# Four operand sums of a Strassen-like down projection, moved from VectorE to accumulating SBUF-to-SBUF transfers

## Chip, cores, metric

One NeuronCore of a Trainium2 chip runs the whole kernel. The metric is device time in microseconds, the median over runs of the same program. A profiled execution gives the trace; its times count from the first instruction (the span's start). Engines are named as in the profile: PE (TensorE matmul), PEld (its weight loads), DVE (VectorE), ACT (ScalarE), POOL (GpSimd), SP (SyncE). POOL and SP issue DMA transfers; those that accumulate into their destination are issued by POOL here.

## What is computed

One layer of a streaming encoder on 512 positions of 1024 channels, in float32. The part that matters here is the gated feed-forward block at the end, with 2816 hidden channels:

```python
h2 = rms_norm(x, norm_ffn[l])
act = jax.nn.silu(jnp.einsum('bsd,df->bsf', h2, w_ffn_gate[l])) * jnp.einsum('bsd,df->bsf', h2, w_ffn_up[l])
x = x + jnp.einsum('bsf,fd->bsd', act, w_ffn_down[l])
```

Before it come a combined input projection, a pooling mixer, a gated linear recurrence and stick-breaking attention, merged by gates, and an output projection. None of these is touched.

## The kernel before

Activations are held with channels on the 128 partitions and positions along the free dimension. A float32 product is made of three matmuls in a rounded 32-bit format: each operand is split into a high part (an ACT copy that rounds) and a low part (DVE: operand minus high part), and hi x hi, hi x lo and lo x hi are accumulated. A split of a weight set therefore costs an ACT copy and a DVE subtraction of 128x1024; a split of an activation block costs the same two of 128x512 for each chunk.

Large products use seven half-size products in place of eight (a Strassen-Winograd scheme). Sums of weights are formed in SBUF by accumulating transfers on POOL's queue or on DVE; sums of activations are formed on DVE.

**The feed-forward block.** The gate and up products run in eleven steps `c` (0 to 10, `DOWN` = 11), each giving `acts[c]`: a tile of 128 x 2 x 512, where the middle index is one of two 128-channel chunks. `finish_act` (L1404) ends the seven products of a step with `S4` for the first chunk and `S3` for the second. It multiplies both factors by `rb2`, the reciprocal RMS per position formed in `rms2`, applies Silu on ACT and multiplies. The last index of `acts` splits into two halves `j` of H = 256 positions.

**The down projection.** `acts[0]` is multiplied in the ordinary way (weights `fd`, tile `ps_d`, L274 to L276). `acts[1]` to `acts[10]` are the Strassen operand: block (i, j) is made of chunks of `acts[1+5i]` to `acts[5+5i]`, positions half j. `ablk(i, kh, j)` gives the pieces for one third `kh` of it: two tiles for kh 0 and 1, one for kh 2, five tiles of 128x512 in all. `split_d2(nm, kh, i, j)` splits such a piece for the product `nm`, on ACT (L1400) and DVE (L1401); its tiles are named `Bd` + product + kh (+ h or l), for instance `BdS20h`. The split of "11" is written during the last step of the gate and up products (`PRE`).

The seven products run in `DORDER` = 11, 12, S1, S2, S3, S4, 22, each with five weight sets n = 0 to 4 in the six pieces of `USE` (two output halves `q`), 120 matmuls of 256 columns at L1633 into `ps_dy` or `ps_dx`. Weight sets are split at L1379 (ACT, `whd`) and L1380 (DVE, `wld`); three split sets can be held at a time. `make_d` writes them ahead of the pieces: ahead of piece p of the first half, up to set p + 2. The raw weights:

- for "11" and "12", "22": sets of "11" are loaded into `DY` (tile `dw`), those of "12" and "22" into three raw buffers (tile `dr`, loaded by SP at L1549 when a buffer comes free);
- for the sums, `DX` is loaded with the block 21 and gets 22 added (S1), later 11 (S2) and 12 (S4); `DY` gets 21 added (S3). Each is an accumulating transfer of 512 KB that POOL issues at L1537, behind the split that has read the set (`NEXT`).

**The sums of activations.** Four sums are formed by `in_place` (L1570) on DVE, in the tiles of `acts` themselves: T1 = (0,0) - (0,1) in the place of (0,0), then T2, T4 in the same place, and T3 in the place of (0,1). Each needs five instructions of 128x512. `LATER[nm]` lists, for each product, which sums and splits are written between its pieces: two entries behind each piece of the first output half, one behind each of the second. T1 and the split of S1 stand in "11", T2 and the split of S2 in "12", T3 and the split of S3 in "S1", the split of S4 and T4 in "S2".

**What sets the order.** Each engine and each DMA queue runs its instructions in the order in which a scheduler put them before the run; semaphores hold an instruction back until its inputs are there, and everything behind it on that engine with it. The scheduler takes instructions by program order among those that it believes to be ready, so that a transfer written late can be issued early. `tc.keep_in_program_order` puts an instruction behind the one that was written just before it on its engine; `in_place` and the DVE part of `split_d2` (for products other than "11" and "12") use it, ACT parts and transfers do not.

Of the kernel before, what the change touches and what calls it, by code (L numbers as in the profile page):

```python
# [31 lines left out]
H = S // 2  # L32
# [34 lines left out]
def layer_kernel(ctx: ExitStack, tc: tile.TileContext, x, xt, vecs, w_in, w_qkv7, w_gate7, w_pool, w_rg, w_ig,  # L67
                 w_branch, w_br7, w_out, w_fd, w_gu7, w_fd7, out):
    nc = tc.nc
    act = nc.scalar.activation  # L70
    dve = nc.vector
# [332 lines left out]
    with ExitStack() as first:  # L404
# [394 lines left out]
        for t in VKQ:  # L799
            ps = {}  # L800
# [451 lines left out]
    with ExitStack() as ffn:  # L1252
# [6 lines left out]
        def small(name, bufs=1, tag=None, dt=F32):  # L1259
            return gp.tile([P, S], dt, tag=tag or name, name=name, bufs=bufs)  # L1260
# [3 lines left out]
        act(onesr, ones, AF.Copy)  # L1264
        sqsum = small("sqsum")
        rb2 = small("rb2")

        x1p = {}
        x1 = []

        def rms2():
# [14 lines left out]
            dve.tensor_tensor(rb2, rb2, ms, ALU.mult)  # L1286
            dve.tensor_scalar(rb2, rb2, -0.5, 1.5, ALU.mult, ALU.add)
            dve.tensor_tensor(rb2, rb2, t, ALU.mult)

# [97 lines left out]
        def ablk(i, kh, j):  # L1387
            return [acts[1 + 5 * i + 2 * kh + n][:, :, j * H:(j + 1) * H] for n in range(2 - kh // 2)]

        def split_d2(nm, kh, i, j):  # L1390

            pin = tc.keep_in_program_order if nm not in ("11", "12") else lambda i: None
            if kh < 2:
                h, l = g4([4, H], f"Bd{nm}{kh}h", F32R), g4([4, H], f"Bd{nm}{kh}l", F32R)
            else:
                t = g4([2, 2, H], f"Bd{nm}{kh}", F32R)
                h, l = t[:, 0], t[:, 1]
            for n, src in enumerate(ablk(i, kh, j)):
                ns = slice(2 * n, 2 * n + 2)
                act(h[:, ns, :], src, AF.Copy)  # L1400
                pin(dve.tensor_tensor(l[:, ns, :], src, h[:, ns, :].bitcast(F32), ALU.subtract))  # L1401
            DB[nm, kh] = h, l

        def finish_act(t, ps, a, sign):  # L1404

            dve.tensor_tensor(t, t, ps, ALU.add)
            for w in range(2):
                dve.tensor_tensor(t[:, w, :], t[:, w, :], rb2, ALU.mult)
            act(t[:, 0, :], t[:, 0, :], AF.Silu, scale=sign)
            if sign > 0:  # L1410
                dve.tensor_tensor(a, t[:, 0, :], t[:, 1, :], ALU.mult)
            else:
                dve.scalar_tensor_tensor(a, t[:, 1, :], sign, t[:, 0, :], ALU.mult, ALU.mult)


        PRE = ("S2", "S4", "22")
# [1 line left out]
        def seven(n):  # L1418
# [39 lines left out]
                dve.tensor_tensor(ah[1], acts[0], ah[0].bitcast(F32), ALU.subtract)  # L1458
            if c == DOWN - 1 and nm in PRE:
                split_d2("11", PRE.index(nm), 0, 0)  # L1460
            if nm == "S4":
                finish_act(tx, X, a[:, 0, :], 1.0)
            if nm == "S3":
                finish_act(ty, Y, a[:, 1, :], -1.0)

        T, Z, ah = {}, {}, []

# [97 lines left out]
                    dadd(m, n, buf)  # L1565
                dfetch(dmade[0] + 2)

        def in_place(dst, sign, op, other):
            return [lambda kh=kh: [tc.keep_in_program_order(
                dve.scalar_tensor_tensor(t, t, sign, o, ALU.mult, op)) for t, o in zip(ablk(dst[0], kh, dst[1]), ablk(other[0], kh, other[1]))]  # L1570
                    for kh in range(3)]

        def both(nm, i, j):
            return [lambda kh=kh: split_d2(nm, kh, i, j) for kh in range(3)]

# [3 lines left out]
                   lambda: [dload("21", n, DX) for n in range(5)],  # L1579
                   lambda: [dadd("22", n, DX) for n in range(5)]] + both("12", 1, 0)[:1])  # L1580

        LATER = {"11": both("12", 1, 0)[1:] + in_place((0, 0), 1.0, ALU.subtract, (0, 1)) + both("S1", 0, 0),
                 "12": in_place((0, 0), -1.0, ALU.subtract, (1, 1)) + both("S2", 0, 0),
                 "S1": in_place((0, 1), -1.0, ALU.add, (1, 1)) + both("S3", 0, 1),
                 "S2": both("S4", 1, 1) + in_place((0, 0), -1.0, ALU.subtract, (1, 0)),
                 "S3": both("22", 0, 0)}

        for e in range(2):
# [128 lines left out]
```

## Time and profile before

| | |
|---|---|
| median of 3 runs | 900.3 us (899.79 to 902.87) |
| the profiled execution | 900.52 us, of which the span of instructions is 898.7 us |
| granted PE clock, mean | 0.998 |
| accumulating transfers of weights in the down projection (POOL, 512 KB) | 20, median 8.0 us from issue to landing |
| loads of weights in the down projection (SP, 512 KB) | 20, medians 6.3 and 5.7 us |
| PE busy from 880 us to the end of the span | 15.35 of 19.00 us |

How to read it: a busy time is the union of an engine's instructions; an engine that is off the path may be idle without cost. In rows of a timeline the first two numbers are start and length in us, and the bracket gives the idle time ahead of the instruction and what ended it. In rows of groups, "x15: 680/682/684" are count and shortest, median and longest duration in ns. In the busy times by stretch, each stretch has its length, then busy time and number of instructions for each engine, then the granted PE clock, the share of the 16 DMA engines' time, and GB/s. In the chain of waits each piece is what the next one waited for.

### The profile page before, as it was taken

To read this page: it belongs to the slowest core of one execution; us is meant where nothing else is said; L and a number is where in the kernel's file an instruction comes from. 1 tells how busy PE (TensorE), PEld (TensorE's weight loads), DVE (VectorE), ACT (ScalarE), POOL (GpSimd) and SP (SyncE) were. 2 spreads that over 40 slices of the span, in tenths; PEclk is the share of its full clock that TensorE was granted. 3 is DMA by queue.
4 is the path that set the end of the run, shared out by engine and by line. 5 is a ranking of instruction groups with operands and counts; after the bars stand their busy time and mean duration, and the time that the engine had idled before them with its cause. 6 is when DMAs were issued, how large, how long until landed. Compare 5 with 4: busy or idle time off the path is not lost.

```text
span 898.7 us, 14578 instructions
## 1 busy us (share of the span) xinstructions
PE 891.1 (99%) x5731; PEld 802.4 (89%) x5731; DVE 736.7 (82%) x937; ACT 532.9 (59%) x747; POOL 106.7 (12%) x150
## 2 busy tenths in 40 slices
PE   9999999999999999999999999999999999998998
PEld 6888778888899888888888988999999999998998
DVE  7897897988786599967887685798888888998974
ACT  7554989556856556555664545655555555654642
POOL 1010002232332101000001100000010100121200
PEclk9999999999999999999999999999999999999999
DMA  9485347798582786634635864836666676887913
GB/s 342 141 309 150 114 132 210 220 299 244 179 262 71 234 234 192 218 118 145 214 93 154 190 179 164 258 81 174 169 148 176 162 169 201 211 210 205 196 39 117
DMA packets 83620, 164.59 MB, mean 183 GB/s; under 512 B 7904, under 2 KB 48864, under 8 KB 83552
## 3 DMA queue, kind: packets, MB, share of 16 engines
q1 hardware_dynamic: 68000, 107.29, 35.9%
q0 software_dynamic: 15408, 56.11, 28.2%
q8 instruction: 45, 0.74, 0.3%
q10 hardware_dynamic: 144, 0.26, 0.1%
q14 instruction: 23, 0.19, 0.1%
HBM read 143.19 MB, written 18.87 MB: 180 GB/s over the span
## 4 chain that ended last, share of the span: by engine, by line
PE 93%; DVE 3%; ACT 2%; DMA 1%; issue 1%; DVEq 0%; ACTq 0%; SPq 0%
PE ps_y L283 13%; PE ps_x L283 10%; PE ps_q L794 7%; PE ps_dy L1633 5%; PE ps_dx L1633 4%; PE ps_br L274 3%; PE ps_br L275 3%; PE ps_br L276 3%; PE ps_bY L1234 2%; PE ps_gy L283 2%; PE ps_gate L697 2%; PE ps_gate L276 2%; PE ps_bX L1234 2%; PE ps_gx L283 2%; PE ps_gate L274 2%; PE ps_gate L275 2%
## 5 line engine op out<-in xcount | busy, mean ns | idle before, releaser
L110 ACT ACTIVATE whi<-raw 128x1024 fp32r<-128x1024 f32 x61 | 64.6, 1059 | 73.3 <-PE ps_br L275 14.7
L111 DVE TENSOR_TENSOR wlo<-raw,whi 128x1024 fp32r<-128x1024 f32 x61 | 74.4, 1220 | 28.9 <-ACT whi L110 28.9
L111 DVE TENSOR_TENSOR wlo<-qw,whi 128x1024 fp32r<-128x1024 f32 x48 | 58.6, 1222 | 20.8 <-ACT whi L110 20.4
L110 ACT ACTIVATE whi<-qw 128x1024 fp32r<-128x1024 f32 x48 | 50.7, 1057 | 33.1 <-PE ps_q L794 18.7
L1379 ACT ACTIVATE wh<-w 128x1024 fp32r<-128x1024 f32 x34 | 36.2, 1064 | 49.4 <-PE ps_x L283 24.7
L1380 DVE TENSOR_TENSOR wl<-w,wh 128x1024 fp32r<-128x1024 f32 x34 | 41.6, 1223 | 7.3 <-ACT wh L1379 6.7
L1380 DVE TENSOR_TENSOR wl_S<-w,wh_S 128x1024 fp32r<-128x1024 f32 x30 | 36.6, 1220 | 12.1 <-ACT wh_S L1379 12.0
L1379 ACT ACTIVATE wh_S<-w 128x1024 fp32r<-128x1024 f32 x30 | 31.8, 1060 | 22.5 <-PE ps_y L283 19.8
L1379 ACT ACTIVATE whdS<-dw 128x1024 fp32r<-128x1024 f32 x20 | 21.3, 1064 | 22.1 <-PE ps_dy L1633 11.1
L1380 DVE TENSOR_TENSOR wldS<-dw,whdS 128x1024 fp32r<-128x1024 f32 x20 | 24.2, 1220 | 6.4 <-ACT whdS L1379 6.3
L1050 DVE TENSOR_TENSOR_SCAN E<-K,ahead 128x512 f32<-128x512 f32 (+3 forms) x32 | 25.3, 812 | 4.4 <-ACT K L1046 4.4
L274 PE MATMUL ps_br<-yHH,whi 128*128 128x512 f32 x64 | 25.3, 395 | 0.0
L274 PE MATMUL ps_lru<-HH,whi 128*128 128x512 f32 x64 | 25.2, 394 | 0.0
L274 PE MATMUL ps_br<-yph,whi 128*128 128x512 f32 x64 | 25.2, 394 | 0.0
L274 PE MATMUL ps_pool<-HH,whi 128*128 128x512 f32 x64 | 25.2, 393 | 0.0
L274 PE MATMUL ps_gate<-HH,whi 128*128 128x512 f32 x64 | 25.0, 391 | 0.0
L276 PE MATMUL ps_gate<-HH,wlo 128*128 128x512 f32 x64 | 25.0, 391 | 0.0
L275 PE MATMUL ps_br<-ypl,whi 128*128 128x512 f32 x64 | 25.0, 391 | 0.0
L276 PE MATMUL ps_br<-yph,wlo 128*128 128x512 f32 x64 | 25.0, 391 | 0.0
L275 PE MATMUL ps_br<-yHL,whi 128*128 128x512 f32 x64 | 25.0, 390 | 0.0
L276 PE MATMUL ps_br<-yHH,wlo 128*128 128x512 f32 x64 | 25.0, 390 | 0.0
L275 PE MATMUL ps_pool<-HL,whi 128*128 128x512 f32 x64 | 25.0, 390 | 0.0
(768 smaller groups left out, 3540.0 us busy)
## 6 DMA issues: line engine op xcount, KB each, us to landing
w<-in_w_gu_dram SPq DMA_DIRECT2D x44, 512.0 KB, 6.6
raw<-in_w_in_dram SPq DMA_DIRECT2D x31, 512.0 KB, 5.2
qw<-in_w_qkv_dram SPq DMA_DIRECT2D x24, 512.0 KB, 6.5
w<-in_w_gu_dram POOLq DMA_DIRECT2D x20, 512.0 KB, 7.3
dw<-in_w_down_dram POOLq DMA_DIRECT2D x20, 512.0 KB, 8.0
raw<-in_w_branch_dram SPq DMA_DIRECT2D x16, 512.0 KB, 4.2
qw<-in_w_qkv_dram POOLq DMA_DIRECT2D x12, 512.0 KB, 7.8
qd<-r POOLq DMA_DIRECT2D x12, 512.0 KB, 7.8
```

Of the source, the lines that this page charges most:

```text
L110: act(hi, raw, AF.Copy)
L111: dve.tensor_tensor(lo, raw, hi.bitcast(F32), ALU.subtract)
L274: nc.tensor.matmul(ps, lh, rh, start=start, stop=False, skip_group_check=skip)
L275: nc.tensor.matmul(ps, lh, rl, start=False, stop=False, skip_group_check=skip)
L276: nc.tensor.matmul(ps, ll, rh, start=False, stop=stop, skip_group_check=skip)
L283: nc.tensor.matmul(o, a_[a][:, w, k, :], b_[b][:, k, :], start=first and n == k == 0, stop=last and n == 2 and k == 3, skip_group_check=True)
L794: nc.tensor.matmul(ps[:, a, :], b_[:, k, ts_], a_[:, kk, :], start=first and n == k == 0, stop=n == 2 and k == 3, skip_group_check=True)
L1050: dve.tensor_tensor_scan(E[:, c0:c0 + n][:, ::-1], K[:, c0 + 1:c0 + n + 1][:, ::-1], ahead[:, S - n:][:, ::-1], 0.0, ALU.mult, ALU.add)
L1234: nc.tensor.matmul(o, ah[x_][:, w, k, :], b[k][y_], start=first_ and n == k == 0, stop=n == 2 and k == 3, skip_group_check=True)
L1379: act(h, src, AF.Copy)
L1380: dve.tensor_tensor(l, src, h.bitcast(F32), ALU.subtract)
L1633: nc.tensor.matmul(o, a_[a][:, w, k0 + k, :], b_[b][:, k, :], start=first and i == k == 0, stop=last and i == 2 and k == nk - 1, skip_grou ...
```

## The change

All four sums become accumulating transfers from SBUF to SBUF, issued by POOL: `dma_sum(dst, kh, other)` adds the block `other` into the block `dst`, one transfer of 128x512 (256 KB) for each tile. The transfers add, so two of the four blocks are written negated: `rbn` holds `rb2` with the second half of the positions negated (two ACT copies of 128x256 in `rms2`, in the place of `sqsum`), and `finish_act` multiplies the second factor by `rbn`; for steps from 6 on the sign of the product is turned as well. Blocks (0,1) and (1,0) then hold negated values. The splits "S2" and "12" read their block negated (ACT with a scale of -1, DVE with a scalar_tensor_tensor).

The places in the program change too: T1 is written directly behind the split of "11" for each kh, during the last step of the gate and up products; T2 behind the split of S1 for each kh, in "11"; T3, the split of S2 and T4 together for each kh, in "12". The lists for "S1" and "S2" keep splits alone.

```diff
+        rbn = sqsum
...
+            act(rbn[:, :H], rb2[:, :H], AF.Copy)
+            act(rbn[:, H:], rb2[:, H:], AF.Copy, scale=-1.0)
...
+        def dma_sum(dst, kh, other):
+            for t, o in zip(ablk(dst[0], kh, dst[1]), ablk(other[0], kh, other[1])):
+                nc.gpsimd.dma_start(t, o, accum_op=ALU.add)
...
             for n, src in enumerate(ablk(i, kh, j)):
                 ns = slice(2 * n, 2 * n + 2)
+                if nm in ("S2", "12"):
+                    act(h[:, ns, :], src, AF.Copy, scale=-1.0)
+                    pin(dve.scalar_tensor_tensor(l[:, ns, :], src, -1.0, h[:, ns, :].bitcast(F32), ALU.mult,
+                                                 ALU.subtract))
+                    continue
...
-        def finish_act(t, ps, a, sign):
+        def finish_act(t, ps, a, sign, first):
...
-            for w in range(2):
-                dve.tensor_tensor(t[:, w, :], t[:, w, :], rb2, ALU.mult)
+            for w, r in enumerate((rb2, rbn)):
+                dve.tensor_tensor(t[:, w, :], t[:, w, :], r, ALU.mult)
             act(t[:, 0, :], t[:, 0, :], AF.Silu, scale=sign)
-            if sign > 0:
+            if (sign > 0) == first:
                 dve.tensor_tensor(a, t[:, 0, :], t[:, 1, :], ALU.mult)
             else:
-                dve.scalar_tensor_tensor(a, t[:, 1, :], sign, t[:, 0, :], ALU.mult, ALU.mult)
+                dve.scalar_tensor_tensor(a, t[:, 1, :], -1.0, t[:, 0, :], ALU.mult, ALU.mult)
...
             if c == DOWN - 1 and nm in PRE:
                 split_d2("11", PRE.index(nm), 0, 0)
+                dma_sum((0, 0), PRE.index(nm), (0, 1))
...
-        def in_place(dst, sign, op, other):
-            return [lambda kh=kh: [tc.keep_in_program_order(
-                dve.scalar_tensor_tensor(t, t, sign, o, ALU.mult, op)) for t, o in zip(ablk(dst[0], kh, dst[1]), ablk(other[0], kh, other[1]))]
-                    for kh in range(3)]
...
-        LATER = {"11": both("12", 1, 0)[1:] + in_place((0, 0), 1.0, ALU.subtract, (0, 1)) + both("S1", 0, 0),
-                 "12": in_place((0, 0), -1.0, ALU.subtract, (1, 1)) + both("S2", 0, 0),
-                 "S1": in_place((0, 1), -1.0, ALU.add, (1, 1)) + both("S3", 0, 1),
-                 "S2": both("S4", 1, 1) + in_place((0, 0), -1.0, ALU.subtract, (1, 0)),
+        LATER = {"11": both("12", 1, 0)[1:] + [lambda kh=kh: (split_d2("S1", kh, 0, 0), dma_sum((0, 0), kh, (1, 1)))
+                                               for kh in range(3)],
+                 "12": [lambda kh=kh: (dma_sum((0, 1), kh, (1, 1)), split_d2("S2", kh, 0, 0), dma_sum((0, 0), kh, (1, 0)))
+                        for kh in range(3)],
+                 "S1": both("S3", 0, 1),
+                 "S2": both("S4", 1, 1),
                  "S3": both("22", 0, 0)}
```

More of the change, by code (lines that the diff above doesn't have):

```diff
@@ L1460, in seven @@
                 split_d2("11", PRE.index(nm), 0, 0)
+                dma_sum((0, 0), PRE.index(nm), (0, 1))
             if nm == "S4":
-                finish_act(tx, X, a[:, 0, :], 1.0)
+                finish_act(tx, X, a[:, 0, :], 1.0, c < 6)
             if nm == "S3":
-                finish_act(ty, Y, a[:, 1, :], -1.0)
+                finish_act(ty, Y, a[:, 1, :], -1.0, c < 6)
         T, Z, ah = {}, {}, []
```

## The prediction, as put on record

> **What bounds the kernel now.** I read the page first, then the waits of PE, the busy times by stretch for the down projection, PE's timeline there, and last the chain of waits in that stretch.
>
> ```profile
> span 898.7 us, 14578 instructions
> ...
> PE 891.1 (99%) x5731; PEld 802.4 (89%) x5731; DVE 736.7 (82%) x937; ACT 532.9 (59%) x747; POOL 106.7 (12%) x150
> ```
>
> PE is busy for 99% of the span, so VectorE time alone is worth nothing; only a stretch where PE is short of operands can be improved. The waits of PE name the one place behind the start where it stands still.
>
> ```profile
> PE ps_dx L1633 <- ACT whd L1379: 1.7, 2, 0.9
> ...
> PE ps_dx L1633 <- DVE wld L1380: 0.8, 1, 0.8
> ```
>
> L1633 is the down projection, ps_dx in its second product ("12"), and whd, wld are the two halves of its split weights. The busy times by stretch show what this place costs:
>
> ```profile
> core 0: us, PE busy (x) PEld busy (x) DVE busy (x) ACT busy (x) POOL busy (x), PEclk, DMA share, GB/s
> ...
> 784.00:800.30 16.30, 16.30 (x96) 14.45 (x95) 16.24 (x24) 8.70 (x13) 2.56 (x3) 1.00 0.95 252
> 800.30:802.20 1.90, 1.90 (x18) 1.90 (x17) 1.90 (x3) 1.06 (x1) 1.53 (x3) 1.00 0.00 0
> 802.20:817.60 15.40, 14.54 (x127) 14.35 (x126) 13.66 (x20) 5.88 (x8) 2.75 (x4) 1.00 1.05 223
> 817.60:826.60 9.00, 7.43 (x49) 7.03 (x48) 7.64 (x10) 6.73 (x9) 0.00 (x1) 0.81 0.58 204
> 826.60:857.30 30.70, 30.70 (x273) 30.70 (x272) 28.48 (x37) 19.18 (x26) 8.44 (x10) 1.00 0.93 172
> 821.10:824.40 3.30, 3.30 (x17) 3.30 (x17) 3.30 (x6) 2.72 (x5) 0.00 (x0) 0.50 0.63 174
> ```
>
> From 826.6 PE runs undisturbed: 30.7 us / 273 = 0.1125 us a matmul. At that pace 802.2 to 817.6 would hold 137 matmuls (there are 127) and 817.6 to 826.6 would hold 80 (there are 49). The 41 missing ones are 4.6 us: the most that this change can win, 0.5%. Part of it is the clock: from 821.1 to 824.4 it is 0.50, and 17 matmuls ran where 29 fit, so 1.4 us went there. The rest are three gaps:
>
> ```profile
> 809.96 0.51 PE L1633 MATMUL ps_dx<-Bd,whd 128*128 128x256 f32 x2 [0.85 <-ACT whd L1379]
> ...
> 818.98 0.39 PE L1633 MATMUL ps_dx<-Bd120h,whd 128*128 128x256 f32 x1 [0.81 <-ACT whd L1379]
> ...
> 820.24 0.39 PE L1633 MATMUL ps_dx<-Bd120h,wld 128*128 128x256 f32 x1 [0.76 <-DVE wld L1380]
> ```
>
> The last two, and the slow clock behind them, come from one chain (start, length, what):
>
> ```profile
> 794.79 5.77 PE ps_dy L1633 x49
> ...
> 801.69 2.41 DVE act L1570 x4
> ...
> 808.84 1.15 DVE wld L1380
> ...
> 810.04 7.72 DMA dr<-in_w_down_dram
> ...
> 817.87 1.07 ACT whd L1379
> ...
> 818.96 1.24 DVE wld L1380
> ```
>
> Four in-place sums on VectorE (L1570, this is T1) delay the weight split at 808.84; the split frees a buffer; the load of the fourth weight set of "12" starts in it at 810.04, lands 7.72 us later, and PE waits for its two splits. After 820 nothing but PE is in the chain.
>
> ```profile
> 820.24 20.70 PE ps_dx L1633 x166
> 840.95 27.20 PE ps_dy L1633 x240
> ...
> 891.95 3.41 PE ps_dx L1633 x30
> ```
>
> So a delay of "12" moves the end by as much.
>
> **The change part by part.** *Removed:* the twenty in-place sums.
>
> ```profile
> L1570 DVE SCALAR_TENSOR_TENSOR act<-act,act x15: 680/682/684, 813.4 to 850.8; 128x512 f32<-128x512 f32 x15
> L1570 DVE SCALAR_TENSOR_TENSOR act<-act x5: 682/683/684, 801.6 to 805.2; 128x512 f32<-128x512 f32 x5
> ```
>
> 20 x 0.682 = 13.6 us leave VectorE. Only T1's 2.4 us lie on the chain above. With them gone the fourth weight set is issued near 807.6 and lands near 815.4; ACT 1.07 and VectorE 1.24 put both splits at 817.7, ahead of 818.2, when PE would come to them without its gap. That wins 0.81 + 0.76 + 1.4 = 3.0 us. The gap of 0.85 at 809.96 stays: there ACT waits for a buffer that PE gives back. What is late next is PE itself.
>
> *Signs:* the negated scale rbn is two ACT copies of 128x256, once.
>
> ```profile
> L1301 ACT ACTIVATE hn<-x,vt 128x256 f32<-128x256 f32 x16 | 7.1, 494 | 0.0
> ```
> ```profile
> 591.57 0.63 ACT L1438 ACTIVATE tx<-tx 128x512 f32<-128x512 f32 x1 [1.35 <-DVE tx L1437]
> ```
>
> 2 x 0.49 = 1.0 us beside an ACT idle time of 1.35 us just behind the place where rb2 is done, with no PE wait there: nothing, and 1.0 us if the cover went. Negated splits and the swapped forms in finish_act replace a tensor_tensor by a scalar_tensor_tensor of the same shape and back; both take 0.68 us in these rows' shape, so nothing.
>
> *Added:* four sums of five transfers each (two, two, one for kh 0, 1, 2), each 128x512 f32, 256 KB in 1 KB rows, all on POOL's queue, where so far the weights are accumulated.
>
> ```profile
> 774.07 0.84 POOL L1537 DMA_DIRECT2D dw<-in_w_down_dram  x1 [6.59 <-DVE wl_S L1380]
> ...
> 800.67 3.57 POOL L1537 DMA_DIRECT2D dw<-in_w_down_dram  x4 [12.86 <-DMA dw<-in_w_down_dram]
> 805.53 0.85 POOL L1537 DMA_DIRECT2D dw<-in_w_down_dram  x1 [1.29 <-DVE wld L1380]
> 826.60 0.84 POOL L1537 DMA_DIRECT2D dw<-in_w_down_dram  x1 [20.22 <-ACT whdS L1379]
> ```
>
> An issue takes 0.85 us of POOL, 17 us for twenty; POOL has the time. Its queue goes in order: the four issues at 800.67 had stood 12.86 us behind one load. What counts is the DMA engines. Of the transfers issued from 800.67 to 805.53 (512 KB each) the time to landing is, and the DMA time from 803 to 809.5, when only they ran:
>
> ```profile
> DMA to landing us min/median/max: 5.5/9.5/12.1
> ```
> ```profile
> q0 software_dynamic: 347, 1.29, 101.9%
> ```
>
> 6.5 us x 1.019 for 1.29 MB is 5.1 us a MB: 2.7 us for 512 KB, 1.35 us for 256 KB. The first lands at 800.67 + 5.5 = 806.2, the fourth three slots later at 814.3, the last 12.1 us after 805.53. An accumulating transfer from SBUF to SBUF is in the trace too:
>
> ```profile
> L1221 POOL DMA_DIRECT2D m<-bt x3: 842/842/850, 502.9 to 517.1; - x3
> ...
> DMA to landing us min/median/max: 4.5/7.0/7.9
> ```
>
> It is no cheaper by much than one from DRAM (4.5 against 5.5 at the least). No row shows one with 1 KB rows. Bounds: 1.04 us (256 KB at the 252 GB/s of 784 to 800.3, the fastest mixed rate above) and 2.7 us (price by row, not by byte: as much as 512 KB). I take 1.35, from the rows of the same operation.
>
> The Trainium skill ("DMA: Bandwidth & Descriptors", section "Anatomy of one DMA — SWDGE (gpsimd) path") has another price: 2.0 us plus the bytes over 436 GB/s for a transfer that GpSimd issues. By it (an estimate) a sum lands 2.6 us after its issue, and the result is that of the second rival below; but the same formula gives 3.2 us for 512 KB, where this trace has 5.5 to 12.1.
>
> *Where they fall.* T1 follows the split of "11", which is in the trace:
>
> ```profile
> 776.60 1.28 DVE L1401 TENSOR_TENSOR Bd110l<-act,Bd110h 128x512 fp32r<-128x512 f32 x2
> ```
>
> The DMA share is 0.95 from 784 to 800.3 and 1.05 from 802.2 to 817.6; between lie 1.9 free us. T1 (five transfers, 6.75 us) is issued from 777.9 on and so pushes what is behind it by 6.75 - 1.9 = 4.85 us. VectorE's S1 splits take the place of T1's sums (801.69); T2's first four follow them, near 803 to 806 (an estimate), behind the four adds of 800.67: they land at 814.3 + 4.85 + 4 x 1.35 = 824.5. In the kernel before T2 was done on VectorE by 815.9 (L1570 at 813.4, four times).
>
> *Who waits.* The split of S2 reads T2, on ACT and then VectorE, and both go in order. Before:
>
> ```profile
> 817.87 1.06 ACT L1379 ACTIVATE whd<-dr 128x1024 fp32r<-128x1024 f32 x1 [7.97 <-DMA dr<-in_w_down_dram]
> 818.84 1.14 ACT L1400 ACTIVATE BdS20h<-act 128x512 fp32r<-128x512 f32 x2
> ```
>
> The program now has the S2 splits of kh 0 and 1 ahead of the fourth weight split; before, only T2's first sums stood there. The order of an engine is settled ahead of the run, by when an input is believed to be there; ACT's 7.97 us on a load shows that this belief takes loads to be faster than they are. I therefore expect BdS20h and BdS21h ahead of this whd. Then whd starts at 824.5 + 1.14 = 825.6 and not at 817.87: 7.8 us later, and with it VectorE's wld, PE's restart (the clock drops as before) and the end. The 3.0 us are not won.
>
> Behind that, T3 and T4 (13.5 us) meet a DMA share of 0.93 from 826.6. T2's rest, T3 and T4 end near 840; the first add for S2, so far issued at 826.6, then lands near 844, and PE comes to S2 at 840.95 + 7.8 = 848.8 with 2.3 us of splits ahead of it. That fits; 2 us more would not.
>
> **Sum.** Profiled execution 900.5 us (span 898.7 and 1.8 around it; median of the runs 900.3): 900.5 + 7.8 = **908.3 us**. At 1.04 us a transfer T1 and T2 cost 2.4 us less: 905.5 (T2 at 821.8). At 2.7 they cost 12.2 more: 920.5.
>
> **The rivals.** *1, faster: the S2 splits are queued behind the last weights of "12".* Then T2 has until S2's turn at 840.95, no wait is added, and VectorE's relief counts: 900.5 - 3.0 = 897.5, at best 895.9. It holds from the point where T2 lands by about 816 (818.2 less 1.07 and 1.14) or ACT has whd first. For it speaks that before ACT had this order; against it, that then T2 waited on VectorE, which is gone. Chance 0.15.
> *2, faster: the sums don't queue.* If they landed in the 4.5 us of the fastest m<-bt, T2 would be there by 810: 897.5 too. The 9.5 us median speaks against it. Chance 0.03.
> *3, slower still: T3 goes ahead of T2.* T3 needs only that T1 has landed, and transfers start as soon as their input is free:
>
> ```profile
> 771.87 0.34 SPq L1549 DMA_DIRECT2D dr<-in_w_down_dram  x1
> ```
>
> This load of the first set of "12" stands in the program behind the first piece of "11", which PE starts at 794.79 (chain): at least 23 us later. T3's first four transfers ahead of T2's add 5.4 us, and POOL stands until T1 has landed: 913.7, with the fifth 915. Chance 0.25.
> *4, price by row:* 920.5. Chance 0.05.
> *5, a wait of under 3 us more,* for instance if only kh 0's split stands ahead, on cheap transfers: 898 to 903. Chance 0.10.
>
> **How the numbers follow.** The forecast has 0.42, from 905.5 to 911 (up to 3 us more if the S1 split of kh 2, which waits for T1's last transfer, holds up ACT in "11"). A measurement of this kernel tells about 0.3% (2.7 us) from no change. Faster by that: rivals 1 and 2, 0.18. Within it: 0.10. Slower: 0.42 + 0.25 + 0.05 = 0.72. The range from 896.5 to 917 leaves out rival 4 and the tails; slower cases alone would be 905 to 917.
>
> **What would show it.** Right: ACT idle before BdS20h or BdS21h, ended by a DMA on act, and PE idle 8 us or more in "12" near 818, no idle time in S1 to 22. T1's transfers take 1.3 us each in the DMA; T2's take 15 us or more to landing. Wrong: whd of the fourth set ahead of BdS20h on ACT (rival 1), T3 ahead of T2 on POOL (rival 3), PE idle in S2 (the adds for S2 late behind T4).

## Result, and the profile after

The change makes the kernel slower: 921.4 us (median of 5 runs, 920.25 to 923.48) against 902.8 us (median of 5 runs of the kernel before beside it, 899.79 to 902.87; the 900.3 known to the forecast was that of three of them). The ratio is 1.022, with a 95% interval from 1.020 to 1.0242. The forecast of 908.3 us had the sign right and was 13 us short; 921.4 lies outside its range. The profiled execution after took 923.48 us, of which the span is 921.4.

PE's waits after (what it waited for: us in total, times, longest) answer to the two rows of before:

```profile
PE ps_dx L1645 <- ACT whd L1383: 16.8, 2, 9.8
PE ps_dx L1645 <- DVE wld L1384: 1.9, 3, 0.8
```

Before it was 1.7 and 0.8. Both long waits stand ahead of weights of "12", and in both ACT was the engine that came last. ACT's timeline there (start, length, instruction, and in the bracket the idle time ahead of it and what ended it) shows why:

```profile
815.05 0.63 ACT L1413 ACTIVATE BdS<-act 128x512 fp32r<-128x512 f32 x1 [11.56 <-DMA act<-act]
815.58 1.99 ACT L1383 ACTIVATE whd<-dr 128x1024 fp32r<-128x1024 f32 x2
832.31 0.63 ACT L1409 ACTIVATE BdS20h<-act 128x512 fp32r<-128x512 f32 x1 [14.74 <-DMA act<-act]
833.65 0.63 ACT L1409 ACTIVATE BdS20h<-act 128x512 fp32r<-128x512 f32 x1 [0.71 <-DMA act<-act]
834.19 1.04 ACT L1383 ACTIVATE whd<-dr 128x1024 fp32r<-128x1024 f32 x1
```

ACT stands still twice, 11.56 and 14.74 us, each time on a transferred sum: first on the last part of T1 (the split of S1, kh 2), then on T2 (the split of S2, kh 0). The weight splits `whd` behind each start as soon as ACT is free; their weights were there. Why the sums came so late is in POOL's timeline:

```profile
782.88 2.68 POOL L1396 DMA_DIRECT2D act<-act  x2
...
786.48 2.72 POOL L1396 DMA_DIRECT2D act<-act  x2
...
795.45 1.18 POOL L1396 DMA_DIRECT2D act<-act  x1 [5.34 <-DMA act<-act]
798.02 1.18 POOL L1396 DMA_DIRECT2D act<-act  x1 [1.39 <-DMA act<-act]
801.55 1.16 POOL L1396 DMA_DIRECT2D act<-act  x1 [2.36 <-DMA act<-act]
802.96 1.18 POOL L1396 DMA_DIRECT2D act<-act  x1 [0.24 <-DMA act<-act]
...
804.23 2.01 POOL L1396 DMA_DIRECT2D act<-act  x1
...
815.55 1.18 POOL L1396 DMA_DIRECT2D act<-act  x1 [8.39 <-DMA act<-act]
816.25 3.14 POOL L1552 DMA_DIRECT2D dw<-in_w_down_dram  x3
817.93 6.28 POOL L1396 DMA_DIRECT2D act<-act  x4
```

L1396 is `dma_sum`. The first four (782.88, 786.48) are T1's kh 0 and 1. The next four (795.45 to 802.96) are **T3's**, not T1's or T2's: the scheduler put them ahead, and each stands on POOL until a transfer of T1 has landed (5.34 + 1.39 + 2.36 + 0.24 = 9.3 us). Only behind them comes T1's last part (804.23). T3's last part at 815.55 stands 8.39 us for the landing of that one, and behind it stand three weight adds and T2's first four, at 817.93. The chain of waits (start, length, what) is made of these landings:

```profile
786.48 14.78 DMA act<-act
...
804.23 10.79 DMA act<-act
...
825.18 16.35 DMA act<-act
```

The stretches of the two stalls, and the rest of the run behind them (length, then busy time and instructions of PE, PEld, DVE, ACT, POOL, granted PE clock, DMA share, GB/s):

```profile
809.70:816.60 6.90, 0.00 (x0) 0.00 (x0) 0.89 (x2) 1.55 (x3) 1.05 (x2) 0.64 0.93 172
816.60:825.50 8.90, 8.11 (x48) 7.64 (x48) 3.26 (x4) 0.97 (x2) 8.84 (x10) 0.70 0.93 193
825.50:835.20 9.70, 0.02 (x1) 0.00 (x0) 0.00 (x0) 2.17 (x4) 0.86 (x1) 0.67 1.13 217
847.10:917.80 70.70, 70.70 (x602) 70.67 (x600) 45.41 (x51) 31.15 (x36) 7.57 (x9) 1.00 0.57 132
```

and the last of these in the kernel before:

```profile
827.20:895.30 68.10, 68.10 (x602) 67.95 (x600) 50.66 (x61) 32.36 (x38) 7.84 (x10) 1.00 0.55 123
```

In the first and the third of these stretches PE stands still; they are the two waits of 16.8 us in all. Its clock fell within each stall and stayed low for some us behind it. From 847.10 on, 602 matmuls took 70.7 us and not 68.1.

One table carries the rest of this document: the time from the first matmul of a product to the first of the next, by the instructions of PE in each trace (us; "rest" is S3, S4 and 22 to PE's end). Undisturbed, a product takes 13.6 us.

| kernel | "11" | "12" | S1 | S2 | rest | PE's end |
|---|---|---|---|---|---|---|
| before | 14.1 | 18.5 | 13.6 | 13.6 | 41.0 | 895.35 |
| after | 21.2 | 30.5 | 14.1 | 14.1 | 42.6 | 917.97 |
| e1_signs | 14.5 | 19.5 | 13.6 | 13.6 | 41.0 | 897.41 |
| e2_t1_only | 14.3 | 19.7 | 13.6 | 13.6 | 41.0 | 897.05 |
| e3_t3_pinned | 14.2 | 25.9 | 18.5 | 16.4 | 41.0 | 910.83 |
| e4_t2_dve | 20.7 | 18.4 | 13.6 | 18.8 | 42.6 | 908.83 |
| e5_t34 | 14.1 | 18.6 | 16.7 | 17.3 | 41.0 | 902.47 |
| e9_t12 | 14.4 | 25.8 | 13.6 | 13.6 | 41.0 | 903.15 |
| e10_t12_late | 14.1 | 19.2 | 16.9 | 14.4 | 41.0 | 900.55 |
| e6_again | 14.4 | 17.6 | 22.8 | 18.8 | 41.0 | 909.38 |
| e8_stores | 15.4 | 20.2 | 17.4 | 17.3 | 41.0 | 906.57 |
| e13_t12_late_held | 14.8 | 18.2 | 14.1 | 14.5 | 41.8 | 898.79 |
| e7_t1_kh01 | 14.1 | 16.6 | 14.1 | 14.1 | 42.6 | 897.19 |
| e14_dve_held | 14.8 | 14.7 | 13.6 | 15.7 | 41.7 | 896.02 |
| e11_t1_held | 14.1 | 13.6 | 13.6 | 14.6 | 41.8 | 892.98 |

After against before: 7.2 us more in "11", 12.0 in "12", 2.7 behind it, and 0.8 that PE came later to "11". Before rounding these add up to the 22.6 us between the two ends of PE. (These are the two profiled executions, 923.48 and 900.52 us; the medians are 18.6 us apart.)

### The profile page after: what moved, and what is told of

It reads as the page before. It is cut to its first block, busy times and chain, and to the rows that moved or that the text cites. A ratio compares the mean times of both kernels' runs of the same rounds, so it can differ in the third digit from the quotient of the medians.

```text
span 921.4 us, 14606 instructions
## 1 busy us (share of the span) xinstructions
PE 897.1 (97%) x5731; PEld 807.5 (88%) x5731; DVE 725.4 (79%) x917; ACT 533.1 (58%) x749; POOL 131.0 (14%) x170
## 4 chain that ended last, share of the span: by engine, by line
PE 87%; DMA 6%; DVE 2%; ACT 2%; POOL 1%; issue 1%; SPq 0%; POOLq 0%; DVEq 0%; ACTq 0%
PE ps_y L283 12%; PE ps_x L283 10%; PE ps_q L794 7%; DMA act<-act 5%; PE ps_dy L1645 4%; PE ps_dx L1645 4%; PE ps_br L274 3%; PE ps_br L275 3%; PE ps_br L276 3%; PE ps_gate L697 2%; PE ps_bY L1234 2%; PE ps_gy L283 2%; PE ps_gate L276 2%; PE ps_bX L1234 2%; PE ps_gx L283 2%; PE ps_gate L274 2%
## 5 line engine op out<-in xcount | busy, mean ns | idle before, releaser
L110 ACT ACTIVATE whi<-raw 128x1024 fp32r<-128x1024 f32 x61 | 64.6, 1058 | 68.9 <-PE ps_br L275 14.7
L1383 ACT ACTIVATE whdS<-dw 128x1024 fp32r<-128x1024 f32 x20 | 21.2, 1059 | 24.4 <-PE ps_dy L1645 13.2
L1396 POOL DMA_DIRECT2D act<-act x20 | 26.7, 1889 | 29.8 <-DMA act<-act 17.7
L1384 DVE TENSOR_TENSOR wld<-dr,whd 128x1024 fp32r<-128x1024 f32 x10 | 12.1, 1222 | 20.8 <-ACT whd L1383 20.8
L1552 POOL DMA_DIRECT2D dw<-in_w_down_dram x20 | 23.4, 1272 | 31.2 <-DVE wldS L1384 15.7
L1377 POOL DMA_DIRECT2D w<-in_w_gu_dram x10 | 8.4, 844 | 120.7 <-ACT ty L1466 103.2
```

The source lines that it names most:

```text
L110: act(hi, raw, AF.Copy)
L1383: act(h, src, AF.Copy)
L1384: dve.tensor_tensor(l, src, h.bitcast(F32), ALU.subtract)
L1396: nc.gpsimd.dma_start(t, o, accum_op=ALU.add)
```

## The experiments

Theory A: it is the *order*. ACT stands in its queue behind splits of T1 and T2, and these land late because POOL stands in its queue. Theory B: it is the *time of the DMA engines*; twenty sums of 1.35 us each (the forecast's price) are 27 us more, and the weights come later whatever the order. Theory C: the negated forms cost.

**e1_signs**: the signs of the change, with all four sums as plain additions on VectorE in the old places.

```diff
-                dma_sum((0, 0), PRE.index(nm), (0, 1))
...
+        def in_place(dst, other):
+            return [lambda kh=kh: [tc.keep_in_program_order(
+                dve.tensor_tensor(t, t, o, ALU.add)) for t, o in zip(ablk(dst[0], kh, dst[1]), ablk(other[0], kh, other[1]))]
+                    for kh in range(3)]
...
+        LATER = {"11": both("12", 1, 0)[1:] + in_place((0, 0), (0, 1)) + both("S1", 0, 0),
+                 "12": in_place((0, 0), (1, 1)) + both("S2", 0, 0),
+                 "S1": in_place((0, 1), (1, 1)) + both("S3", 0, 1),
+                 "S2": both("S4", 1, 1) + in_place((0, 0), (1, 0)),
```

> The signs alone: blocks written negated, rbn, negated splits and the swapped forms as in the change, but all four sums formed on VectorE (as plain additions) at the places they had before. Theory A (order: ACT stands in its queue behind splits that read T1 and T2, which land late because POOL's queue stands in order and the DMA engines are full) and theory B (bandwidth: 27 us more of DMA time delays the weights, whatever the order) both expect 899 to 903 us, no change. Theory C (the negated forms cost) expects over 905.

Measured: 902.1 us, ratio 0.9996 (0.9976 to 1.0015). The signs cost nothing; theory C falls.

**e2_t1_only**: T1 by transfer, T2 to T4 as in e1_signs. This and the next diffs of the lists are against e1_signs.

```diff
+                dma_sum((0, 0), PRE.index(nm), (0, 1))
...
-        LATER = {"11": both("12", 1, 0)[1:] + in_place((0, 0), (0, 1)) + both("S1", 0, 0),
+        LATER = {"11": both("12", 1, 0)[1:] + both("S1", 0, 0),
```

> T1 alone by transfers, T2 to T4 on VectorE. Theory A: without T3 ahead of it, T1's last transfer is issued near 790 instead of 804 and lands near 803 to 806, so the first of the two stalls of PE (7.0 us before the first set of 12) shrinks to 0 to 3 us and the second is gone: 898 to 904 us, and the chain through T1 on VectorE (2.4 us) is gone too. Theory B: a quarter of the added DMA time, a quarter of the loss: 905 us.

Measured: 903.1 us, ratio 1.0023 (1.0005 to 1.0041), in A's range. VectorE is relieved of T1, yet "12" takes 19.7 us. The chain of this kernel says where the relief went:

```profile
790.19 17.32 DMA act<-act
...
807.54 0.64 ACT BdS L1413
...
809.41 1.23 DVE wld L1384
...
810.65 9.02 DMA dr<-in_w_down_dram
```

T1's last part takes 17.32 us to land. The splits of S1's kh 2 wait for it on ACT and VectorE, and behind them stands the weight split (809.41; 808.84 before) that frees the buffer of the fourth load (810.65; 810.04 before). One wait has taken the place of the other.

**e3_t3_pinned**: the change, with T3 held on POOL behind what is written ahead of it.

```diff
-                nc.gpsimd.dma_start(t, o, accum_op=ALU.add)
+                i = nc.gpsimd.dma_start(t, o, accum_op=ALU.add)
+                if dst == (0, 1):
+                    tc.keep_in_program_order(i)
```

> The change with T3's transfers held behind what is written before them on POOL (T2 among it); bytes and transfers as in the change. Theory A: POOL no longer stands for T1's last part ahead of T2; T1 complete near 806 and not 815, T2 from 822 to 826 and not 832 to 836; one stall of about 8 us in 12 is left: 907 to 911 us. Theory B: same bytes, same time: 918 to 923.

Measured: 916.7 us, ratio 1.0161 (1.0132 to 1.019): above A's range, just below B's. ACT's timeline:

```profile
807.50 0.63 ACT L1415 ACTIVATE BdS<-act 128x512 fp32r<-128x512 f32 x1 [4.47 <-DMA act<-act]
...
821.44 0.63 ACT L1411 ACTIVATE BdS20h<-act 128x512 fp32r<-128x512 f32 x1 [11.42 <-DMA act<-act]
822.77 0.63 ACT L1411 ACTIVATE BdS20h<-act 128x512 fp32r<-128x512 f32 x1 [0.70 <-DMA act<-act]
823.31 1.04 ACT L1383 ACTIVATE whd<-dr 128x1024 fp32r<-128x1024 f32 x1
...
825.50 0.63 ACT L1411 ACTIVATE BdS21h<-act 128x512 fp32r<-128x512 f32 x1 [0.63 <-DMA act<-act]
```

The stall in "11" is gone (14.2 us in the table): T1's last part lands at 807.5 and not at 815.0. T2's first four land by 825.5 and not by 836.3. So T3's place on POOL made the stall in "11" and put T2 off by 11 us; a stall of 8.3 us in "12", behind T2, is left. And S1 and S2 now lose 4.9 and 2.8 us. ACT stands for parts of T3 ahead of weight splits of S1, and then for the first weight add of S2:

```profile
840.84 0.63 ACT L1415 ACTIVATE BdS31h<-act 128x512 fp32r<-128x512 f32 x1 [3.76 <-DMA act<-act]
...
852.39 1.06 ACT L1383 ACTIVATE whdS<-dw 128x1024 fp32r<-128x1024 f32 x1 [3.88 <-DMA dw<-in_w_down_dram]
```

**e4_t2_dve**: T2 on VectorE, the other three by transfer, T3 free to go ahead. It is e2_t1_only with:

```diff
-                 "12": in_place((0, 0), (1, 1)) + both("S2", 0, 0),
-                 "S1": in_place((0, 1), (1, 1)) + both("S3", 0, 1),
-                 "S2": both("S4", 1, 1) + in_place((0, 0), (1, 0)),
+                 "12": in_place((0, 0), (1, 1)) + [lambda kh=kh: (dma_sum((0, 1), kh, (1, 1)), split_d2("S2", kh, 0, 0), dma_sum((0, 0), kh, (1, 0)))
+                        for kh in range(3)],
+                 "S1": both("S3", 0, 1),
+                 "S2": both("S4", 1, 1),
```

> T1, T3 and T4 by transfers as in the change, T2 on VectorE. Theory A: the second stall (9.8 us, behind T2's landing) is gone, the first (7.0 us, behind T1's last part at 815) stays, with half of the time at the slow clock: 907 to 911 us. Theory B: three quarters of the loss: 916.

Measured: 912.4 us, ratio 1.0114 (1.0078 to 1.0149), above A's range by 1 us. The stall behind T2 is gone ("12" 18.4), the one behind T1 stays ("11" 20.7), and S2 loses 5.2:

```profile
813.79 0.63 ACT L1413 ACTIVATE BdS<-act 128x512 fp32r<-128x512 f32 x1 [11.02 <-DMA act<-act]
```

So the two stalls have two causes: the first goes with T3's place (e3_t3_pinned), the second when T2 is not a transfer (here).

**e5_t34**: T3 and T4 by transfer, T1 and T2 on VectorE: the lists of e4_t2_dve, with T1 as in e1_signs.

```diff
-                dma_sum((0, 0), PRE.index(nm), (0, 1))
...
-        LATER = {"11": both("12", 1, 0)[1:] + both("S1", 0, 0),
+        LATER = {"11": both("12", 1, 0)[1:] + in_place((0, 0), (0, 1)) + both("S1", 0, 0),
```

> T3 and T4 by transfer, T1 and T2 as additions on VectorE; T3's first four stand on POOL ahead of the last weight adds for S1. Theory A (it is the order: ACT stands behind splits of T1 and T2, which land late): no split of "11" or "12" reads a transferred sum, so both stalls in "12" are gone: 899 to 904 us, what is above 902 being waits of the S1 to S3 adds behind T3 and T4. Theory B (it is the DMA time that the sums take): the ten sums still take 13.5 us or more of all 16 engines while the weights of "12" and S1 are fetched: about 911.

Measured: 907.0 us, ratio 1.0049 (1.0024 to 1.0074): between the two. "12" is that of before, as A said; S1 and S2 lose 3.1 and 3.7 us, more than A allowed.

**e9_t12**: T1 and T2 by transfer, T3 and T4 on VectorE. This is the forecast's own step, alone. Against e2_t1_only:

```diff
-        LATER = {"11": both("12", 1, 0)[1:] + both("S1", 0, 0),
-                 "12": in_place((0, 0), (1, 1)) + both("S2", 0, 0),
+        LATER = {"11": both("12", 1, 0)[1:] + [lambda kh=kh: (split_d2("S1", kh, 0, 0), dma_sum((0, 0), kh, (1, 1)))
+                                               for kh in range(3)],
+                 "12": both("S2", 0, 0),
```

> T1 and T2 by transfer, T3 and T4 as additions on VectorE. This is the step that the prediction called likeliest, by itself: no T3 can go ahead of T2, and no T3 or T4 is late. Theory A (order; ACT stands behind the S2 splits that read T2): T2's first four land near 825, ACT's split of the fourth weight set of "12" comes some 7 us late, "12" takes 25 to 26 us and not 18.5: 908 to 911 us. Theory B (the sums' DMA time delays the weights): 13.5 us of DMA time, half of it ahead of the fourth load: 906 to 911. The two are told apart by the next kernel.

Measured: 911.7 us (908.33 to 913.25, 4 runs), ratio 1.0106 (1.0076 to 1.0137), just above both ranges; the profiled execution is the 908.33. In it ACT's timeline and the table agree with the forecast to about a microsecond: T2's fourth part lands at 825.57, "12" takes 7.3 us more than before and PE ends 7.8 us later.

```profile
821.51 0.63 ACT L1409 ACTIVATE BdS20h<-act 128x512 fp32r<-128x512 f32 x1 [11.40 <-DMA act<-act]
822.85 0.63 ACT L1409 ACTIVATE BdS20h<-act 128x512 fp32r<-128x512 f32 x1 [0.70 <-DMA act<-act]
823.38 1.04 ACT L1383 ACTIVATE whd<-dr 128x1024 fp32r<-128x1024 f32 x1
...
825.57 0.63 ACT L1409 ACTIVATE BdS21h<-act 128x512 fp32r<-128x512 f32 x1 [0.63 <-DMA act<-act]
```

**e10_t12_late**: the same transfers in the same order, with the S2 splits behind the last weight splits of "12" on ACT.

```diff
-                 "12": both("S2", 0, 0),
+                 "12": [lambda: None] * 6 + both("S2", 0, 0),
...
-                    act(h[:, ns, :], src, AF.Copy, scale=-1.0)
+                    i = act(h[:, ns, :], src, AF.Copy, scale=-1.0)
+                    if nm == "S2":
+                        tc.keep_in_program_order(i)
```

> As e9_t12, same transfers in the same order on POOL, but the S2 splits stand on ACT behind all the weight splits of "12". Theory A: the stall in "12" goes back to the 3 us of the kernel before: 901 to 904 us. Theory B: the transfers are the same, so the time is that of e9_t12.

Measured: 907.9 us, ratio 1.0069 (1.0043 to 1.0094). "12" falls from 25.8 to 19.2 us: that ACT stood behind the S2 splits is shown. But the time, between A's and B's, gains only 3.8 us, since S1 now takes 16.9. The chain goes through T2's last part and the S2 split on ACT that waits for it, ahead of a weight split of S1:

```profile
812.88 20.29 DMA act<-act
...
833.73 1.05 ACT whdS L1383
```

**e6_late_s2** and **e6_again**: e3_t3_pinned with the S2 splits late in the same way (and pinned on ACT as above).

```diff
-                 "12": [lambda kh=kh: (dma_sum((0, 1), kh, (1, 1)), split_d2("S2", kh, 0, 0), dma_sum((0, 0), kh, (1, 0)))
-                        for kh in range(3)],
+                 "12": [lambda kh=kh: dma_sum((0, 1), kh, (1, 1)) for kh in range(3)] + [lambda: None] * 3 +
+                       [lambda kh=kh: (split_d2("S2", kh, 0, 0), dma_sum((0, 0), kh, (1, 0))) for kh in range(3)],
```

> All four sums by transfer, T3 behind T2 as in e3_t3_pinned, and the two S2 splits written behind all the weight splits of "12" instead of ahead of the last ones. Theory A: the stall of 8.3 us behind T2's landing goes, and 903 to 909 us are left by the later waits of S1 and S2 for T3 and T4. Theory B: the weights come as late as in e3_t3_pinned, whatever stands in ACT's queue: 914 to 918.

Measured: 916.7 us, ratio 1.0157 (1.0134 to 1.0181): as B said, and far above A. Its profiled execution was one of 5138 us and shows nothing of this place; e6_again is the same kernel.

> The kernel of e6_late_s2 once more, because its profiled execution took 5138 us (its others 914.9 to 918.2) and shows nothing of the place in question. Theory A, mended after that run's 916 us: "12" takes 19 to 21 us and not 25.9 as in e3_t3_pinned, and the loss has moved to S1 and S2, where the S2 splits and S1 and S2 adds wait for T2, T3 and T4. Theory B: "12" takes 25 us as before.

Measured: 915.4 us, ratio 1.0157 (1.0125 to 1.0188). "12" takes 17.6 us and not 25.9; S1 and S2 take 22.8 and 18.8. B's 25 us for "12" fall, and A's move of the loss to S1 and S2 holds ("12" is even below A's 19 to 21): the order in "12" is mended, and next to nothing is won. PE's waits, and the weight adds of this kernel (KB each, median us from issue to landing, 8.0 before):

```profile
PE ps_dx L1649 <- ACT whdS L1383: 3.7, 2, 2.7
...
PE ps_dy L1649 <- DVE wldS L1384: 1.7, 3, 0.8
```
```profile
dw<-in_w_down_dram POOLq DMA_DIRECT2D x20, 512.0 KB, 14.2
```

So A alone falls: what is not lost in "12" is lost in S1 and S2, where the weight adds come late and ACT still stands for parts of T2 (3.01 us at 829.40) ahead of weights.

**e8_stores**: the sums on VectorE (as e1_signs), and at the twenty places of the transfers a store of 512 KB from `acts` into spare memory, on POOL in program order. Nobody reads the stores.

```diff
+        def load_dma(kh):
+            for n in range(2 - kh // 2):
+                spare.append(dr.tile([P, 2, S], F32, tag=f"spare{len(spare)}", name=f"spare{len(spare)}"))
+                tc.keep_in_program_order(nc.gpsimd.dma_start(spare[-1], acts[6 + 2 * (kh % 2) + n]))
```

> Sums on VectorE as in e1_signs; at the twenty places where the transferred sums stood in the program, POOL issues plain stores of 512 KB into spare memory that nobody reads, held in program order on POOL, with about the DMA time of the sums (1.3 us of all 16 engines each). Theory A: no split waits for them, so 900 to 908 us; what is above 902 is POOL and the DMA engines being busy. Theory B: the weights are delayed as much as by the sums: 915 to 921.

Measured: 911.4 us, ratio 1.0108 (1.009 to 1.0126), between the two. No split waits for these transfers, and they still cost 9 us, most of it in S1 and S2, where PE waits for weights:

```profile
PE ps_dy L1658 <- ACT whdS L1383: 3.6, 1, 3.6
PE ps_dx L1658 <- ACT whd L1383: 3.4, 2, 2.5
```

From 808 to 836 the DMA share was 1.04, and 0.80 in e1_signs. But POOL stood as well. Eleven of the stores were held on it, 19.0 us in all, each until 0.3 us after the eighth transfer before it had landed: in no trace of this case does POOL have more than eight under way. So the first add for S2 was issued at 836.50 and not at 828.72 (e1_signs). That transfers for which nobody waits cost time is B's part; DMA time and POOL's standing are not told apart by this kernel. Nor does it say whether B alone could make 921: the first five stores ran at 768 to 790, ahead of the down projection, and the last ones landed 1.24 us apart, so that the fifteen others take some 18.6 us (an estimate) and not 27.

**e13_t12_late_held**: e10_t12_late with three of the five weight adds for S3 held behind the first three adds for S2. They fill the DMA engines near 800 and are needed near 855.

```diff
+        HELD = (("11", 2), ("11", 3), ("11", 4))
...
-                if nm in NEXT:
+                if nm in NEXT and (nm, n) not in HELD:
                     m, buf = NEXT[nm]
                     dadd(m, n, buf)
+                if nm == "S1" and n < 3:
+                    tc.keep_in_program_order(dadd("21", n + 2, DY))
```

> As e10_t12_late (T1 and T2 by transfer, S2 splits behind the last weights of "12", the same order on ACT), and the three adds for S3 held as in e11_t1_held. If the DMA time of what runs beside the sums is what remains of the loss: T2's last part, which landed at 833.2 in e10_t12_late, lands by 826, S1 takes 14 and not 16.9 us: 901 to 904 us. If it is not: 907 to 909 as e10_t12_late.

Measured: 903.3 us, ratio 1.001 (0.9989 to 1.0031). S1 takes 14.1 us and not 16.9, and no S2 split waits for a sum any more. With the same sums and the same order on ACT, the loss is gone once three weight adds no longer run ahead of T2. That frees the DMA engines and POOL alike: T2's last transfer is issued at 810.11 and not at 812.88. From 798 to 827 their share was, in e10_t12_late and then here (the DMA share is the last number but one):

```profile
798.00:827.00 29.00, 25.91 (x206) 25.30 (x205) 17.99 (x22) 13.09 (x17) 9.90 (x10) 0.94 1.11 240
```
```profile
798.00:827.00 29.00, 26.70 (x208) 25.99 (x208) 17.95 (x23) 13.95 (x19) 6.84 (x7) 0.94 1.03 219
```

**e7_t1_kh01**: of T1 only kh 0 and 1 by transfer, issued first; all else on VectorE. Against e1_signs:

```diff
+                if nm != "22":
+                    dma_sum((0, 0), PRE.index(nm), (0, 1))
...
-        LATER = {"11": both("12", 1, 0)[1:] + in_place((0, 0), (0, 1)) + both("S1", 0, 0),
+        LATER = {"11": both("12", 1, 0)[1:] + both("S1", 0, 0)[:2] + in_place((0, 0), (0, 1))[2:] + both("S1", 0, 0)[2:],
```

> T1 by transfer for kh 0 and 1 alone (four transfers, issued first), the rest of T1 and T2 to T4 on VectorE. Theory A: T1's early parts land by 803, before any split of "11" asks for them; VectorE is relieved of 2.7 us in "11", ACT waits for nothing: 898 to 902 us, faster than before by up to 3 us if the fourth weight set of "12" then starts earlier. Theory B: 5.4 us more DMA time ahead of the fourth set of "12": 904 to 907.

Measured: 900.4 us, ratio 0.9982 (0.9968 to 0.9996), in A's range. ACT splits the fourth weight set of "12" at 816.48 and not at 819.99 (e1_signs), and PE waits only 0.55 us for it; it now waits for the fifth, whose load takes 10.88 us beside the full DMA engines:

```profile
810.30 10.88 DMA dr<-in_w_down_dram
```

**e14_dve_held** and **e11_t1_held**: the three held adds of e13_t12_late_held (the same diff), in e1_signs and in e7_t1_kh01.

> No transferred sum (as e1_signs), only the three adds for S3 held. Tells how much of a gain of e11_t1_held is the held adds' own: if the DMA time is what delays the fourth load of "12", it lands 2 us or more earlier and the kernel takes 898 to 900 us; if VectorE's T1 sums delay it, as the prediction said, 901 to 903 us.

Measured: 900.9 us, ratio 0.9992 (0.9974 to 1.001). The time is in neither range, but the trace tells what delayed the fourth load. It starts at 811.58, no earlier than in e1_signs (811.11), and lands at 814.95 and not at 819.89. ACT's split of it, in e1_signs and then here:

```profile
819.99 1.06 ACT L1383 ACTIVATE whd<-dr 128x1024 fp32r<-128x1024 f32 x1 [9.10 <-DMA dr<-in_w_down_dram]
```
```profile
815.06 1.07 ACT L1383 ACTIVATE whd<-dr 128x1024 fp32r<-128x1024 f32 x1 [3.58 <-DVE wld L1384]
```

So 4.9 us of the delay were the DMA time of the adds beside it. The held adds alone mend "12" (14.7 us and not 19.5); S2 and what follows give 2.8 us back.

> As e7_t1_kh01, and three of the five weight adds for S3 (sets 2 to 4, 512 KB each, needed only near 855 us), which so far run at 798 to 812, are held on POOL behind the first three adds for S2. Theory B's part (DMA time is what is short in "12"): 8.1 us less DMA time ahead of the fifth load of "12", which took 10.88 us in e7_t1_kh01; it lands by 817, "12" takes 13.6 to 15 us and not 16.6: 897 to 899 us, if S2 and S3 do not wait instead. Theory A alone (order): 900 to 902.

Measured: **898.1 us**, ratio 0.9956 (0.994 to 0.9971). This is 0.4% faster than the kernel before. In the stretch of "12" PE has no idle time, 122 matmuls in 13.6 us, and the only waits in the down projection that are listed are two, of 1.0 us together:

```profile
809.40:823.00 13.60, 13.60 (x122) 13.60 (x121) 13.02 (x17) 7.81 (x10) 1.53 (x2) 1.00 0.65 203
```
```profile
PE ps_dy L1652 <- DVE wldS L1384: 1.0, 2, 0.5
```

## Why the prediction was right and wrong

The forecast had the direction and the kind of the stall in "12" right. It failed on where the transfers fall: on POOL's order ahead of "12", and on what comes late behind it.

**The bound of 4.6 us: right.** No kernel here wins more.

**The 3.0 us of VectorE's relief: right in size, half right in the reason.** With four of T1's transfers issued first, the fourth load comes earlier, as forecast, but the kernel gains only 0.2% (e7_t1_kh01), since the fifth load is then late. With three adds held as well it gains 0.4%, 3.3 us (e11_t1_held); the held adds alone give 0.1%, which is not clear of nothing (e14_dve_held). The forecast put the fourth set's lateness down to VectorE's sums alone; its load's DMA time was the larger part (e14_dve_held). The gap at 809.96, which was to stay, is gone in e7_t1_kh01 and e11_t1_held. That the change itself doesn't win the 3.0 us was right too; the reason in "11" was one that the forecast did not have, T1's own last part (e2_t1_only).

**Signs for nothing: right** (e1_signs).

**The price of a sum, 1.35 us: right.** T2's landings in e9_t12 follow each other at 821.51 and 822.85. The time from issue to landing of the twenty in the kernel after was:

```profile
DMA to landing us min/median/max: 3.8/11.3/16.4
```

The Trainium skill ("DMA: Bandwidth & Descriptors", section "Anatomy of one DMA — SWDGE (gpsimd) path") gives 2.0 us plus the bytes over 436 GB/s, by which an estimate for one of these is 2.6 us. This trace does not agree, not even at its least; from 3.8 to 16.4 us for transfers of one size, the wait among other transfers is the larger part here. Two smaller numbers were off. An issue of a sum cost POOL 1.16 us at the least and 1.5 at the median, not 0.85. And at 1.04 us a transfer T1 and T2 cost 2.8 us less, not 2.4; the 905.5 is worked out with 2.8.

**Who waits: right.** The S2 split of kh 0 stands ahead of weights of "12" on ACT, even ahead of the third set. With the order that the forecast assumed (e9_t12), T2's fourth part landed at 825.6 (824.5 forecast), and PE's end moved by 7.8 us (7.8 forecast). That the two agree so closely is in part luck: this is the fastest of four executions, and the medians are 10.6 us apart.

**"Where they fall": this step failed.** It put T2's issues near 803 to 806, behind the four adds of 800.67. They came at 817.93, because T3 stood ahead of them. That was rival 3, at 0.25, and its mechanism is what happened; but it was priced at the DMA time of T3 (5.4 us, 913.7). What T3 costs is that POOL *stands* until T1 lands, 9.3 us ahead of T1's last part and 8.39 us ahead of T2. The forecast said that POOL stands until T1 has landed, and gave it no time. PE's end missed the forecast by 14.8 us: 7.2 in "11", 4.2 in "12", 2.7 behind it and 0.8 ahead of "11".

**"Up to 3 us more" for the S1 split of kh 2: mis-sized.** It became the first stall, 7.0 us of PE and 7.2 us of "11", since T3's four stood ahead of T1's last part as well. In e3_t3_pinned T3's share is gone from both stalls, and the time falls by some 5 us only.

**"That fits; 2 us more would not": failed, and was hidden by the rest.** e3_t3_pinned has all twenty transfers in the order that the forecast assumed. There PE ends 15.5 us later than before: 7.4 us of it stand in "12", as forecast, and 7.7 in S1 and S2, which the forecast put at nothing. The last part of T4 lands at 849.8, where the forecast had the sums end near 840, and the first add for S2 at 852.3 and not near 844. With the S2 splits late as well the two products lose 14.4 us (e6_again), and with T3 and T4 alone 6.8 (e5_t34). In the kernel after they lose only 0.5 each, the slower pace of all its later products; presumably the 16.8 us in which PE stood had let the transfers go ahead.

**What was left out or taken too short:** the half clock behind a stall was taken as before, 3.3 us, and was 10.2 us twice; the slower pace behind it (below) is worth 2.7 us.

Of the theories, neither stands alone. Shown is: T3's place makes the first stall and lengthens the second (e3_t3_pinned), the second goes without T2's transfer (e4_t2_dve) or with the S2 splits behind the weights (e9_t12 against e10_t12_late), transfers for which nobody waits cost time (e8_stores), and the loss from T1 and T2 goes when three other transfers are moved out of their way (e13_t12_late_held). Not shown is how that last part divides between the DMA engines and POOL's standing. Nor can it be told in one number how much of the 18.6 us is order and how much DMA time, since what one gives back the other takes (e6_again).

## What to carry to other kernels

A transfer that needs another's landing blocks every transfer behind it on its queue (9.3 and 8.39 us here): look where the scheduler will hoist it to, and price the standing of the queue as well as the bytes. Before work is moved from an idle-looking path to the DMA engines, read their share in that very stretch (0.95 to 1.05 here): moving four of the five parts of one sum, with three other transfers put off, won 0.4%; moving all four sums lost 2.2%. When a wait is removed and the time stays, look for the next late operand in the later stages, product by product.

## What was not expected of the hardware

**The half clock.** It set in within each of the two stalls, 2.0 and 3.2 us after PE fell idle, and lasted some 10 us each time; the matmuls that ran there started 0.21 us apart:

```profile
811.60:821.90 10.30, 4.51 (x19) 4.22 (x20) 4.16 (x5) 2.53 (x3) 6.35 (x9) 0.50 0.87 153
828.70:838.90 10.20, 3.16 (x13) 2.86 (x14) 3.64 (x6) 4.30 (x6) 1.28 (x2) 0.50 1.15 199
```

The forecast knew only the 3.3 us of before, behind two gaps of 0.8 us. The Trainium skill ("TensorE: Matmul & The Clock Gate", section "Part 1: The HAM clock gate (the "warmup" mystery)") has the clock fall behind an idle window of about 3.4 us and come back after one busy window. The lengths here, 3.3 and 10.2 to 10.3, are near one and three such windows; that gaps of 0.8 us can be enough, as before, is not in that section. Nor are they always: in e7_t1_kh01 two gaps of 0.75 and 0.76 us (822.39 and 823.65) were not followed by a lower clock. What decides was not found.

**Two paces at full clock.** From the last pause in the down projection to the end, PE starts a matmul of 256 columns every 113.3 ns in the profiles of before, e1, e2, e3 and others, and every 117.8 ns in those of after, e4 and e7, at a granted clock of 1.00 in both (the rows of 847.10 and 827.20 above: 70.7 and 68.1 us for 602). From "12" on it changes only where PE has paused or its clock has been low. It is worth 2.7 us of this result, and perhaps part of the scatter between runs of one kernel (e9_t12's profiled execution is 908.33, its others 911.55 to 913.25). What sets it was not found.

**Eight transfers under way.** POOL never has more than eight transfers issued and not landed, in any of these traces (six at most in the kernel before); in e8_stores the next one stood until the eighth before it had landed. So twenty more transfers cost not only their DMA time: what stands behind them on POOL is issued later. Whether the chip or the kernel's framework sets the eight is not shown.

**One very slow execution.** In the 5138 us of e6_late_s2, PE alone was slow: a matmul every 640 ns in the down projection, where the same kernel has 113. VectorE and ScalarE were busy for 741 and 541 us, against 726 and 533 in e6_again. The profile gives PE's clock as 1.00, but this trace holds no record of the clock at all, where the others do, so it is not known. It occurred once and is unexplained.
